# Scaled fp16 projections in a two-layer diffusion backbone: values, queries and keys, and two loads moved

## The chip, the cores and the metric

The kernel runs as one program on 1 core of one Trainium2 chip. The metric is the time of one execution on the device, in microseconds (us). TensorE (PE) multiplies matrices into PSUM; VectorE (DVE) and ScalarE (ACT) do the elementwise work and move results out of PSUM; GpSimd (POOL), SyncE (SP) and ACT issue DMA transfers. Each engine works through its own list of instructions in the order in which the program holds them.

## The reference: what is computed

Two layers over 1024 latent tokens and 256 context tokens of width 1024, in float32. Layer 0 mixes tokens with Fourier groups and a Hyena convolution, layer 1 with neighbourhood attention of 16 heads; both end in a SwiGLU of width 2816. The lines that bear on this change:

```python
def swiglu(u, w_gate, w_up, w_down):
    return (jax.nn.silu(u @ w_gate) * (u @ w_up)) @ w_down

def mixer_na(u_lat, u_ctx, w_qkv, w_out, rpb, with_ctx_out):
    heads = lambda t: t.reshape(t.shape[0], t.shape[1], NA_HEADS, NA_HEAD_DIM)
    q, k, v = (heads(t) for t in jnp.split(u_lat @ w_qkv, 3, axis=-1))
    kc, vc = (heads(t) for t in jnp.split(u_ctx @ w_qkv[:, D_MODEL:], 2, axis=-1))
    y_lat = neighbourhood_attention(q, k, v, kc, vc, rpb).reshape(B_, L, D_MODEL) @ w_out
```

In layer 1, `u_lat` and `u_ctx` are the normalised and modulated streams, `rms_norm(h) * (1 + scale) + shift`. Its context output isn't needed, so context tokens have keys and values there, and no queries.

## The kernel before, in words

**Two parts for each operand.** A matrix product is made of three: an operand is split into a high part, rounded to a shorter format, and a low part, the rest; high by high, high by low and low by high are added up in PSUM. In most of the kernel both parts are `float32r` (`split`, L352 on ACT and L354 on DVE). The feed-forward products use fp16 parts instead (`split_scaled`, L1885 and L1886): weights and activations are first multiplied by factors that keep them in fp16's range, found from the largest absolute values (`scan` and `bound` sum absolute values on ACT, `scale_x`, `scale_w` and a reduction over partitions on POOL make the factor), and the results are multiplied by the inverse.

**Stages in order of time.** (1) Layer 0's mixer and its output projection. (2) Layer 0's feed-forward: context's gate and up products, then the latent ones by a Winograd-like scheme of 7 products for 2 by 2 blocks (`wino_steps`, matmuls on L2032), in 11 groups `i`, each with one gate and one up matrix pair. (3) `down` for layer 0: seven passes `p` over 11 operand pairs (matmuls on L2279), then context's own down product, 22 steps `kb` of 24 matmuls (L2401). (4) `values`: V for 10 blocks of tokens, 4 weight tiles `kp` for each of four accumulation groups. (5) `attention`: 64 items (a head, half the rows, two column chunks) in three stages each (scores, transposes of the probabilities, the product with V), with `attn_prep` of the next pair of heads woven between them: K for latent and context tokens and Q, 24 matmuls for each of 5 pieces. All of their matmuls go through the helper at L348. (6) The output projection, layer 1's feed-forward and `down`.

**What sets the order.** A tile framework records the program and a list scheduler orders each engine's instructions; buffers come from pools (21 tiles of 4 KB a partition in `p4`, 35 of 2 KB in `p2`, 4 of tag `ws` for staged weights, two each of tags `wh` and `wl` for split ones, the last also used as four `hl` tiles, each holding both fp16 parts). `follow(x)` tells the scheduler to place what comes next after instruction `x`; `next(g)` in the loops takes the next piece of a side job `g`.

**Around the change.** In the feed-forward's group `i`, `sums` (L2085) loads four tiles of the down weights and makes from them the four sums that Winograd needs, writes them to DRAM (L2093 to L2096) and bounds them (L1965, ACT). `ahead` is a `scan` over layer 1's gate and up weights (L1854 on ACT, loads on ACT's queue, L336), four pieces to a group. In `down`, `operands` (L2257) loads two tiles, 256 KB each, and splits them (L2269 ACT, L2270 DVE); `mark` (L2342) remembers the last load and split of pass 5, and context's down weights (512 KB each, L2394) are placed behind `mark`. Plain loads are issued by SP (L333), spills by POOL (L339).

## Time and profile before

| what | value |
|---|---|
| time, median of 3 runs | 2844.2 us (2842.24 to 2845.08) |
| profiled execution, its own time | 2844.23 us |
| its span in the trace | 2842.5 us |
| mean granted TensorE clock | 0.982 |
| busy: PE, PE weight loads, DVE, ACT, POOL | 2722.5, 1839.6, 2128.6, 1594.8, 508.4 us |
| feed-forward of layer 0, latent part | 913 to 1318 us |
| `down` of layer 0, seven passes / context's part | 1318 to 1538 / 1538 to 1598 us |
| `values` | 1598 to 1708 us |
| attention with its projections | 1708 to about 2180 us |
| feed-forward of layer 1 and `down` | 2234 to 2842 us |

A row of a matmul in the trace lasts from its start to its modelled end, so rows overlap: what a stream of matmuls costs is the distance from start to start. Weight loads (PEld) run beside matmuls. Some matmul records are missing from a trace, above all for fp16, where weight loads are instructions of their own and are counted in full. "landed" is when a DMA's data had arrived. "`<-`" behind idle time names what ended it.

### The profile page before, as it was taken

What the parts mean: (1) busy time and instruction counts of PE and PEld (TensorE: products, weight loads), DVE (VectorE), ACT (ScalarE), POOL (GpSimd) and SP (SyncE); (2) the same over time, 40 slices, a digit from 0 to 9 for tenths busy, and PEclk for the clock granted to TensorE, in tenths of its full rate; (3) what the DMA queues carried; (4) which work ended last, traced back from release to release, by engine and by line L of the source; (5) the groups of instructions that cost most, each with busy time, mean ns of one, the idle gap of its engine ahead of it and who ended that gap; (6) DMA issues with size and microseconds to landing.
All of it is one profiled execution on the core that took longest, in us unless ns stands there. A gap on an engine that the chain in (4) does not pass through costs nothing. (4 is left out here: it accounts for less than half of the span.)

```text
span 2842.5 us, 44453 instructions
## 1 busy us (share of the span) xinstructions
PE 2722.5 (96%) x15570; PEld 1839.6 (65%) x15570; DVE 2128.6 (75%) x3849; ACT 1594.8 (56%) x2957; POOL 508.4 (18%) x817
## 2 busy tenths in 40 slices
PE   6999889999999999999999999999999999999998
PEld 3877677888898444444445888888887544444444
DVE  5678788868877898886897736777787876776774
ACT  3533334543488665666656526778775555565653
POOL 2110223351100011112021002323222012221000
PEclk9999899999999999999999999999999999999999
DMA  7344726766645677787997436878775245655872
GB/s 264 99 159 144 220 93 196 230 200 221 227 165 181 236 270 255 255 320 265 372 318 241 134 115 162 191 187 199 188 261 171 101 142 202 219 207 178 291 231 97
DMA packets 308862, 583.34 MB, mean 205 GB/s; under 512 B 82968, under 2 KB 129754, under 8 KB 308638
## 3 DMA queue, kind: packets, MB, share of 16 engines
q1 hardware_dynamic: 241374, 378.61, 42.1%
q0 software_dynamic: 53760, 158.38, 16.0%
q10 hardware_dynamic: 13504, 43.52, 4.4%
q8 instruction: 122, 2.00, 0.3%
q14 instruction: 102, 0.84, 0.1%
HBM read 433.05 MB, written 119.80 MB: 194 GB/s over the span
## 5 line engine op out<-in xcount | busy, mean ns | idle before, releaser
L2032 PE MATMUL ps<-s,s 128*128 128x512 f16 x2280 | 512.5, 379 | 11.3 <-ACT g L2037 3.3
L2032 PEld LDWEIGHTS <-s 128*128 128x128 f16 x2640 | 257.9, 98 | 327.2 <-issue 16.4
L348 PE MATMUL ps<-s,wh 128*128 128x256 f32 (+1 forms) x1784 | 408.8, 332 | 8.7 <-ACT wh L352 6.0
L348 PEld LDWEIGHTS ps<-s,wh 128*128 128x128 f32 x1784 | 298.5, 191 | 44.3 <-ACT wh L352 8.7
L2279 PE MATMUL ps<-s 128*128 128x512 f16 (+2 forms) x1404 | 321.4, 380 | 5.9 <-ACT s L2269 5.9
L2279 PEld LDWEIGHTS <-s 128*128 128x128 f16 x1716 | 167.1, 98 | 205.5 <-issue 12.4
L348 PE MATMUL ps<-s,wl 128*128 128x256 f32 (+1 forms) x892 | 271.3, 330 | 3.9 <-DVE wl L354 3.9
L2269 ACT ACTIVATE s<-s,c 128x512 f16<-128x512 f32 (+1 forms) x300 | 199.9, 715 | 115.4 <-DMA s<-d 67.8
L348 PE MATMUL pq<-s,wh 128*128 128x512 f32 (+1 forms) x840 | 256.6, 385 | 0.4 <-ACT wh L352 0.4
L348 PE MATMUL ps<-s,s 128*128 128x65 f16 (+4 forms) x2748 | 230.9, 235 | 15.3 <-DMA s<-tk 7.6
L2270 DVE SCALAR_TENSOR_TENSOR s<-s,c,s 128x512 f16<-128x512 f32 (+1 forms) x300 | 210.3, 749 | 45.2 <-ACT s L2269 44.6
L339 POOL DMA_DIRECT2D d<-s x245 | 133.1, 544 | 521.3 <-DVE s L1744 86.1
L2032 PE MATMUL ps<-s,hl 128*128 128x512 f16 x924 | 214.6, 379 | 1.3 <-ACT hl L1885 1.3
L2032 PEld LDWEIGHTS <-hl 128*128 128x128 f16 x1056 | 103.2, 98 | 126.0 <-ACT hl L1885 1.5
L348 PEld LDWEIGHTS ps<-s,wl 128*128 128x128 f32 x892 | 166.7, 190 | 22.6 <-DVE wl L354 5.7
L354 DVE TENSOR_TENSOR wl<-ws,wh 128x1024 fp32r<-128x1024 f32 (+1 forms) x84 | 99.5, 1187 | 89.0 <-ACT wh L352 84.7
L348 PEld LDWEIGHTS pq<-s,wh 128*128 128x128 f32 x840 | 150.5, 190 | 22.8 <-ACT wh L352 1.0
L348 PE MATMUL pq<-s,wl 128*128 128x512 f32 (+1 forms) x420 | 159.3, 380 | 0.0
L352 ACT CAST wh<-ws 128x1024 fp32r<-128x1024 f32 (+1 forms) x84 | 84.5, 1010 | 132.9 <-PE ps L348 82.8
L348 PEld LDWEIGHTS ps<-s,s 128*128 128x128 f32 (+1 forms) x828 | 130.3, 193 | 25.0 <-issue 3.4
L1886 DVE SCALAR_TENSOR_TENSOR s<-t,c,s 128x512 f16<-128x512 f32 x176 | 128.1, 746 | 10.1 <-ACT s L1885 10.1
L1885 ACT ACTIVATE s<-t,c 128x512 f16<-128x512 f32 x176 | 118.6, 713 | 6.0 <-DVE t L2011 4.5
(534 smaller groups left out, 5239.3 us busy)
## 6 DMA issues: line engine op xcount, KB each, us to landing
s<-d SPq DMA_DIRECT2D x326, 256.0 KB, 4.9
d<-s POOLq DMA_DIRECT2D x229, 256.0 KB, 3.5
s<-in_down SPq DMA_DIRECT2D x150, 256.0 KB, 5.6
ws<-in_gate SPq DMA_DIRECT2D x42, 512.0 KB, 4.1
ws<-in_up SPq DMA_DIRECT2D x42, 512.0 KB, 4.8
s<-in_ada_w POOLq DMA_DIRECT2D x34, 512.0 KB, 7.0
d<-s SPq DMA_DIRECT2D x60, 256.0 KB, 2.3
s<-in_ada_w ACTq DMA_DIRECT2D x30, 512.0 KB, 7.7
```

Of the source, the lines that this page charges most:

```text
L339: self.last_ldr = self.nc.gpsimd.dma_start(out, in_).ins
L348: self.last_mm = self.nc.tensor.matmul(o, l, r, start=st, stop=sp).ins
L352: self.last_hi = nc.scalar.copy(hi, src).ins
L354: self.last_lo = eng.tensor_tensor(lo, src, hi.bitcast(F32), SUB).ins
L1885: self.last_hi = self.nc.scalar.activation(hi, src, AF.Copy, scale=s).ins
L1886: self.last_lo = self.nc.vector.scalar_tensor_tensor(lo, src, s, hi, op0=MUL, op1=SUB).ins
L2032: nc.tensor.matmul(ps, x[:, sl], y, start=first and j == 0 and x is wh and y is xh, stop=j == 3 and x is wl, skip_group_check=True)
L2269: self.last_hi = nc.scalar.activation(x, f[:, c:c + 512], AF.Copy, scale=s).ins
L2270: self.last_lo = nc.vector.scalar_tensor_tensor(y, f[:, c:c + 512], s, self.raw_part(x), op0=MUL, op1=SUB).ins
L2279: m = nc.tensor.matmul(acc[j][:, c0:c1], x[:, sl], y[:, xs], start=first and k == 0, stop=last and k == 2, skip_group_check=True)
```

## The change

Three things are done.

1. **V, K and Q are projected from fp16 parts.** The normalised stream of layer 1 (`u1`) is held in fp16 (`new_act16`) and scaled by a factor for the latent and one for the context stream (`scale_u`, made at the end of layer 0's feed-forward from the modulation's rows). The weights `wv`, `wk` and `wq` are split by `weights16` into fp16 parts with a factor each (`scale_p`). For those factors the absolute values of the weights are summed: `wv`'s 8 tiles behind the 44 of `ahead` in layer 0's feed-forward (five pieces to a group instead of four; `up.to(3)` is split off from `up.to(5)` for the fifth), `wk`'s and `wq`'s 16 tiles in `values`, two pieces to each weight tile. The copies out of PSUM multiply by the inverse factors.
2. **Loads for the sums of down's weights** are recorded between the first and second half of the gate's steps, and their arithmetic stays at the group's end, in both layers.
3. **`mark` is taken in pass 6** instead of pass 5: context's down weights are placed behind the last operands of the whole of `down`.

```diff
+    def new_act16(self, pc, b):
+        act = Act()
+        w = WID[pc]
+        t = self.S4(F16, 2048) if pc < 2 else self.S2(F16, 1024)
+        for k in range(4):
+            act.put(k % 2, b + k // 2, pc, t[:, k * w:k * w + w])
+        return act
...
-    def scan(self, key, tiles):
+    def scan(self, tiles, mark):
...
-            with self.follow(self.last_ev):
+            with self.follow(mark()):
                 if k > 1:
-                    nc.scalar.activation(t, t, AF.Abs, accum_out=sums[:, k - 2:k - 1])
+                    nc.scalar.activation(t, t, AF.Abs, accum_out=tiles[k - 2][1])
                 if k < n:
-                    self.lda(t, tiles[k])
+                    self.lda(t, tiles[k][0])
...
+    def scale_u_begin(self):
+        nc = self.nc
+        t = self.cw[:, 20:28]
+        for c in (0, 1):
+            for j in (0, 1):
+                nc.vector.tensor_reduce(t[:, 2 * j + c:2 * j + c + 1], self.ada[(1, c)][:, j * 8:j * 8 + 8], axis=AX, op=MAX,
+                                        apply_absolute_value=True)
+        nc.gpsimd.partition_all_reduce(t[:, 4:8], t[:, 0:4], channels=P, reduce_op=bass.bass_isa.ReduceOp.max)
+        return t
...
+    def scale_p(self, sums, maxes, names, c0):
+        nc = self.nc
+        nc.gpsimd.partition_all_reduce(maxes, sums, channels=P, reduce_op=bass.bass_isa.ReduceOp.max)
...
+    def weights16(self, src, s):
+        st = self.W("ws", "ws")
+        self.ld(st, src)
+        return self.split_scaled(st, self.hl(), s)
...
-        def sums(i):
+        def sums_load(i):
...
+            return t
+
+        def sums(i, t):
+
+            a21, a22, a11, a12 = t
...
-            ahead = self.scan("next", [a[x][1, fb] for x in ("gate", "up") for fb in range(NFB)])
+            sums2 = self.wsc["next"] = self.C(4 * NFB)
+            src = [a[x][1, fb] for x in ("gate", "up") for fb in range(NFB)]
+            ahead = [(x, sums2[:, k:k + 1]) for k, x in enumerate(src)]
+            ahead += [(a["wv"][k // 4, k % 4], self.cws[:, k:k + 1]) for k in range(8)]
+            ahead = self.scan(ahead, lambda: self.last_ev)
...
             g.to(5)
             up.to(1)
+            ks = (2 * i - 6, 2 * i - 5) if l == 1 else (9, 10) if i == 9 else (i,) if i < 9 else ()
+            ks = [(k, sums_load(k)) for k in ks if 0 <= k < n2]
             next(ahead, None)
             g.to(7)
...
+            up.to(3)
+            next(ahead, None)
             up.to(5)
             next(ahead, None)
...
-                if p == 5 and i == n2 - 1:
+                if l == 0 and p == 1 and i == 9:
+                    with self.follow(self.last_lo):
+                        self.scale_p(self.cws[:, 0:8], self.cws[:, 8:16], (("v", 1.0),), 32)
+                if p == 6 and i == n2 - 1:
                     mark = self.last_ld, self.last_hi, self.last_lo
...
-                    wh, wl = self.weights(a["wv"][ch, kp])
+                    wh, wl = self.weights16(a["wv"][ch, kp], self.wsc["v"][0])
...
-            self.aw = self.weights(a["wk"][0])
+            self.aw = self.weights16(a["wk"][0], self.wsc["k"][0])
...
-                    wq = self.weights(a["wq"][pr])
+                    wq = self.weights16(a["wq"][pr], self.wsc["q"][0])
...
-                nc.scalar.copy(dst[own], acc[pc][own, :w])
-                nc.vector.tensor_tensor(dst[other], acc[pc][own, :w], dst[own].bitcast(F32), SUB)
+                s = self.wsc["k"][2 if pc == 2 else 1][own]
+                nc.scalar.activation(dst[own], acc[pc][own, :w], AF.Copy, scale=s)
+                nc.vector.scalar_tensor_tensor(dst[other], acc[pc][own, :w], s, dst[own].bitcast(F32), op0=MUL, op1=SUB)
...
+        qk = self.scan([(a[x][k], self.cws[:, c + k:c + k + 1]) for x, c in (("wk", 16), ("wq", 24)) for k in range(8)],
+                       lambda: self.last_hi)
         for i, _ in enumerate(self.values(u1)):
...
+            for _ in range(2 if i < 9 else 0):
+                next(qk)
```

How the order of instructions moves, at three places. The first is SP's queue at the turn from pass 5 to pass 6 of `down` in layer 0. `s<-in_down` and `s<-d` are the two halves of an operand pair, `ws<-in_down 128x2x512` is one step's weights for context. Before:

```order
L333 DMA s_3128_14292<-d_7511 128x512
L333 DMA s_3128_14292<-d_7466 128x512
L333 DMA ws_14600<-in_down 128x2x512
L333 DMA ws_14643<-in_down 128x2x512
L333 DMA ws_14676<-in_down 128x2x512
L333 DMA ws_14719<-in_down 128x2x512
L333 DMA s_3130_14312<-in_down 128x512
L333 DMA s_3130_14312<-d_7397 128x512
L333 DMA ws_14798<-in_down 128x2x512
L333 DMA ws_14831<-in_down 128x2x512
L333 DMA s_3132_14320<-in_down 128x512
L333 DMA s_3132_14320<-d_7404 128x512
```

After the change the 11 operand pairs of pass 6 follow pass 5's last one directly, and then the context weights; of the pairs the first two and the last two are shown:

```order
L333 DMA s_3128_14323<-d_7511 128x512
L333 DMA s_3128_14323<-d_7466 128x512
L333 DMA s_3130_14343<-in_down 128x512
L333 DMA s_3130_14343<-d_7397 128x512
L333 DMA s_3132_14351<-in_down 128x512
L333 DMA s_3132_14351<-d_7404 128x512
...
L333 DMA s_3157_14551<-in_down 128x512
L333 DMA s_3157_14551<-d_7460 128x512
L333 DMA s_3160_14560<-in_down 128x512
L333 DMA s_3160_14560<-d_7467 128x512
L333 DMA ws_14631<-in_down 128x2x512
L333 DMA ws_14673<-in_down 128x2x512
```

Eight context loads, four of them ahead of pass 6's first operand, have moved behind its last.

The second is SP's queue in one group of layer 0's feed-forward, before:

```order
L333 DMA ws_10210<-in_up 128x1024
L333 DMA ws_10212<-in_up 128x1024
L333 DMA ws_10459<-in_gate 128x1024
L333 DMA s_2515_10079<-in_down 128x512
L333 DMA s_2516_10080<-in_down 128x512
L333 DMA s_2517_10081<-in_down 128x512
L333 DMA s_2518_10082<-in_down 128x512
L333 DMA s_2519_10099<-d_7514 128x512
L333 DMA ws_10461<-in_gate 128x1024
```

and after:

```order
L333 DMA ws_10216<-in_up 128x1024
L333 DMA ws_10218<-in_up 128x1024
L333 DMA s_2510_9991<-in_down 128x512
L333 DMA s_2511_9992<-in_down 128x512
L333 DMA s_2512_9993<-in_down 128x512
L333 DMA s_2513_9994<-in_down 128x512
L333 DMA ws_10467<-in_gate 128x1024
L333 DMA s_2519_10105<-d_7514 128x512
L333 DMA ws_10469<-in_gate 128x1024
```

The four loads for the sums stand ahead of the next group's first gate load, where they stood behind it.

The third is ACT's list at the start of `values` after the change: `hl<-ws` (here L1933) is the high part of a `wv` tile, `s<-in_wk` a load for the sums over `wk`, and L1862 such a sum.

```order
L336 DMA s_3279_15501<-in_wk 128x1024
L336 DMA s_3280_15502<-in_wk 128x1024
L1933 ACTIVATE hl_15507<-ws_15505,c_317 128x1024
L1862 ACTIVATE s_3279_15501,c_319<-s_3279_15501 128x1024
L1862 ACTIVATE s_3280_15502,c_319<-s_3280_15502 128x1024
L336 DMA s_3279_15501<-in_wk 128x1024
L1933 ACTIVATE hl_15558<-ws_15556,c_317 128x1024
L336 DMA s_3280_15502<-in_wk 128x1024
L1862 ACTIVATE s_3279_15501,c_319<-s_3279_15501 128x1024
```

Before the change nothing but splits of weights, copies and the norm's work stood there.

More of the change, by code (lines that the diff above doesn't have):

```diff
@@ L684, in norm_block @@
         nc.scalar.activation(hi, t[:, :w], AF.Identity, bias=sh)
[L685 removed]
+        nc.vector.scalar_tensor_tensor(lo, t[:, :w], sh, self.raw_part(hi), op0=ADD, op1=SUB)
     def norm(self, h, pcs, l, m, act):
@@ L1842, in scale_x @@
         self.xinv = t[:, 0:1]
-    def scan(self, key, tiles):
+    def scan(self, tiles, mark):
         nc = self.nc
         n = len(tiles)
-        sums = self.C(2 * n)
         st = [self.S4() for _ in range(2)]
@@ L1851, in scan, with scale_u @@
             t = st[k % 2]
-            with self.follow(self.last_ev):
+            with self.follow(mark()):
                 if k > 1:
-                    nc.scalar.activation(t, t, AF.Abs, accum_out=sums[:, k - 2:k - 1])
+                    nc.scalar.activation(t, t, AF.Abs, accum_out=tiles[k - 2][1])
                 if k < n:
-                    self.lda(t, tiles[k])
+                    self.lda(t, tiles[k][0])
             yield
-        self.wsc[key] = sums
+    def scale_u_begin(self):
[7 more added lines that the diff above has]
+        return t
+    def scale_u(self, t):
+        nc = self.nc
+        self.uinv = self.cw[:, 28:30]
+        s = self.cw[:, 30:32]
+        nc.vector.scalar_tensor_tensor(self.uinv, t[:, 6:8], 32.0, t[:, 4:6], op0=MUL, op1=ADD)
+        nc.vector.tensor_scalar(self.uinv, self.uinv, 1e-30, 1.0 / 8192.0, op0=MAX, op1=MUL)
+        nc.vector.reciprocal(s, self.uinv)
+        for c in (0, 1):
+            ad = self.ada[(1, c)][:, :16]
+            nc.vector.tensor_scalar(ad, ad, s[:, c:c + 1], None, op0=MUL)
+    def scale_p(self, sums, maxes, names, c0):
+        nc = self.nc
+        nc.gpsimd.partition_all_reduce(maxes, sums, channels=P, reduce_op=bass.bass_isa.ReduceOp.max)
+        for j, (k, f) in enumerate(names):
+            t = self.cw[:, c0 + 4 * j:c0 + 4 * j + 4]
+            nc.vector.tensor_reduce(t[:, 0:1], maxes[:, 8 * j:8 * j + 8], axis=AX, op=MAX)
+            nc.vector.tensor_scalar(t[:, 0:1], t[:, 0:1], 1e-30, 1.0 / 8192.0, op0=MAX, op1=MUL)
+            nc.vector.reciprocal(t[:, 1:2], t[:, 0:1])
+            nc.vector.tensor_scalar(t[:, 2:4], self.uinv, t[:, 0:1], f, op0=MUL, op1=MUL)
+            self.wsc[k] = t[:, 1:2], t[:, 2:3], t[:, 3:4]
+    def weights16(self, src, s):
+        st = self.W("ws", "ws")
+        self.ld(st, src)
+        return self.split_scaled(st, self.hl(), s)
     def either(self, x):
@@ L2152, in bounds @@
         def bounds(i, ts):
+            nonlocal us
             for j, t in enumerate(ts):
@@ L2159, in bounds @@
             hidden.clear()
+            if i == n2 - 2 and l == 0:
+                us = self.scale_u_begin()
             if i == n2 - 2:
@@ L2165, in ffn @@
         self.junk = self.S2(mybir.dt.bfloat16)
-        hidden = []
+        hidden, us = [], None
         prev = None
@@ L2219, in ffn @@
                 nc.vector.reciprocal(dsc, inv)
+                if l == 0:
+                    with self.follow(add):
+                        self.scale_u(us)
             prev = (up, gate)
-            for k in (2 * i - 6, 2 * i - 5) if l == 1 else (9, 10) if i == 9 else (i,) if i < 9 else ():
-                if 0 <= k < n2:
-                    sums(k)
+            for k, t in ks:
+                sums(k, t)
                 if l == 0:
@@ L2435, in values @@
                     t = self.T()
-                    nc.scalar.copy(t, acc[tb])
+                    nc.scalar.activation(t, acc[tb], AF.Copy, scale=self.wsc["v"][2 if tb >= 8 else 1])
                     nc.vector.tensor_reduce(mx[:, ch * 10 + tb:ch * 10 + tb + 1], t, axis=AX, op=MAX,
@@ L2524, in attn_prep @@
                 if pc == 1 and i == 3 and pr < 7:
-                    nxt = self.weights(a["wk"][pr + 1])
+                    nxt = self.weights16(a["wk"][pr + 1], self.wsc["k"][0])
                 yield s
@@ L2529, in attn_prep @@
                 qh, ql = self.S2(F32R), self.S2(F32R)
-                nc.scalar.mul(qh[own], acc[pc][own], 0.125)
-                nc.vector.scalar_tensor_tensor(ql[own], acc[pc][own], 0.125, qh[own].bitcast(F32), op0=MUL, op1=SUB)
+                s = self.wsc["q"][1][own]
+                nc.scalar.activation(qh[own], acc[pc][own], AF.Copy, scale=s)
+                nc.vector.scalar_tensor_tensor(ql[own], acc[pc][own], s, qh[own].bitcast(F32), op0=MUL, op1=SUB)
                 for t in (qh, ql):
@@ L2860, in after2 @@
                 if b % 2 == 0:
-                    u1.t.update(self.new_act(pcs=(pc,), blocks=(b, b + 1)).t)
+                    u1.t.update(self.new_act16(pc, b).t)
                 self.norm_block({b: h3.ap(0, b, pc)}, b, pc, 1, 0, u1, r)
@@ L2872, in run @@
                 next(self.last, None)
-            if i in (8, 10):
+            for _ in range(2 if i < 9 else 0):
+                next(qk)
+            if i in (8, 10, 12):
                 with self.follow(self.last_lo):
@@ L2876, in run @@
                         self.scale_x(1, 3)
+                    elif i == 10:
+                        self.scale_p(self.cws[:, 16:32], self.cws[:, 32:48], (("k", 1.0), ("q", 0.125)), 36)
                     else:
```

2 lines of the change are left out of this document (removed).

## The prediction

> **What bounds the kernel now.** I read the windows by stage first, then for each stage what ended TensorE's idle time, then the timeline for the distance from matmul to matmul.
>
> ```profile
> PE 2722.5 (96%) x15570; PEld 1839.6 (65%) x15570; DVE 2128.6 (75%) x3849; ACT 1594.8 (56%) x2957; POOL 508.4 (18%) x817
> 913.00:1318.00 405.00, 393.90 (x1812) 176.93 (x1813) 342.53 (x633) 260.10 (x518) 62.48 (x116) 1.00 0.74 263
> 1318.00:1538.00 220.00, 214.09 (x969) 102.36 (x967) 179.87 (x322) 125.58 (x195) 32.44 (x61) 0.98 0.89 317
> 1598.00:1708.00 110.00, 110.00 (x491) 91.11 (x489) 48.41 (x86) 36.84 (x57) 0.37 (x1) 1.00 0.38 123
> 1734.00:2140.00 406.00, 391.97 (x3758) 350.11 (x3756) 318.58 (x701) 310.16 (x708) 114.52 (x188) 1.00 0.78 197
> ```
>
> The columns after the stretch and its length are PE, PEld, DVE, ACT and POOL busy, the granted clock, the DMA share and GB/s. In `values` (1598 to 1708) PE is never idle and everything else is lightly used; in attention PE is idle for 14 of 406 us. So a matmul that is shortened there shortens the path, as long as the other engines keep up: DVE and ACT are at 78% and 76% in attention. The feed-forward is PE's too, with 11 us of idle time.
>
> **Context's down weights.** The one large hole in PE's work in this half of the kernel lies at the start of pass 6:
>
> ```profile
> 1499.68 1.24 PE L2279 MATMUL ps<-s 128*128 128x512 f16 x5
> 1504.64 5.28 PE L2279 MATMUL ps<-s 128*128 128x512 f16 x12 [3.72 <-ACT s L2269]
> 1511.93 1.02 PE L2279 MATMUL ps<-s 128*128 128x512 f16 x4 [2.01 <-ACT s L2269]
> 1512.79 0.98 PE L348 MATMUL pq<-c,tk 128*128 128x1 f32 x8
> ACT s L2269 <- DMA s<-in_down: 5.8, 2, 5.1
> 1477.89 2.12 SPq L333 DMA_DIRECT2D ws<-in_down  x4
> 1480.10 0.65 SPq L333 DMA_DIRECT2D s<-in_down  x1
> 1488.64 3.26 SPq L333 DMA_DIRECT2D ws<-in_down  x2
> 1497.49 0.42 SPq L333 DMA_DIRECT2D s<-in_down  x1
> ws<-in_down SPq DMA_DIRECT2D x8, 512.0 KB, 11.1
> 2597.69 2.75 PE L2032 MATMUL ps<-s,s 128*128 128x512 f16 x12
> 2600.28 4.91 PE L2032 MATMUL ps<-s,hl 128*128 128x512 f16 x22
> ```
>
> PE waits for ACT's split, which waits for the operand's load, which SP issued behind context loads of 512 KB; those took 11.1 us to land, and SP could issue the third pair only at 1497.49. An fp16 matmul of 512 columns costs 0.216 us: 12 between 2597.69 and 2600.28. The last of the five at 1499.68 is done by about 1500.8; until 1512.79 there are 16 matmuls, 3.5 us of work. The hole is 12.0 - 3.5 = **8.5 us**. With the context loads behind pass 6's last operand its cause is gone. What is late next would be context's first weights. Pass 5's last operand was issued ahead of 1477.89, 23 us before the pass ended at 1500.8. Pass 6 takes 132 x 0.216 = 28.5 us from there, to 1529; at the same lead its last pair is issued about 1506, and the context loads follow, some 20 us ahead of context's first matmul. I take the full 8.5 us; the low end is 4, should half of the wait return at 1530.
>
> **V, K and Q.** The cost now, from the first matmul of a stretch to that of the next:
>
> ```profile
> 1653.37 0.61 PE L348 MATMUL ps<-wh,s 128*128 128x512 f32 x2
> 1656.77 0.61 PE L348 MATMUL ps<-wh,s 128*128 128x512 f32 x2
> 1707.99 0.62 PE L348 MATMUL pq<-s,wh 128*128 128x512 f32 x2
> 1718.65 0.39 PE L348 MATMUL pq<-s,wl 128*128 128x512 f32 x1
> 1718.88 0.40 PE L348 MATMUL pq<-s,wh 128*128 128x256 f32 x2
> 1721.63 0.28 PE L348 MATMUL pq<-s,wl 128*128 128x256 f32 x1
> 1721.86 0.71 PE L348 MATMUL pq<-s,wh 128*128 128x512 f32 x2
> 1733.42 0.63 PE L348 MATMUL pq<-s,wh 128*128 128x512 f32 x2
> 1563.28 21.12 PE L2401 MATMUL ps<-s,hl 128*128 128x256 f16 x192
> ```
>
> V: 15 matmuls in 3.40 us, 0.2267 each. K: 47 steps in 10.66 us, 0.2268. K of context: 23 steps of 256 columns in 2.75 us, 0.1196. Q, whose moving operand is read in pieces of 16 columns: 48 in 11.56 us, 0.2408. In fp16 the first two should cost 0.216, the third 0.110 (192 in 21.1 us). The trace has no fp16 stream read in pieces of 16; Q can gain nothing (0.2408 again) or all (0.216), and I take K's gain of 11 ns, since the pieces should cost fp16 what they cost now.
> V: 480 x 10.8 ns = 5.2 us. K: 8 x 48 x 11 ns = 4.2. Context's K: 8 x 24 x 9.6 ns = 1.8. Q: 384 x 11 ns = 4.2 (0 to 9.5). Together **15.4 us** (11.2 to 20.7).
>
> [...]
>
> The weight loads that become instructions of their own, 1440, run beside the matmuls:
>
> ```profile
> L348 PEld LDWEIGHTS ps<-wh,s x224: 187/188/192, 1598.1 to 1707.5; 128*128 128x128 f32 x112
> L2401 PEld LDWEIGHTS <-hl x528: 95/98/181, 1538.9 to 1598.0; 128*128 128x128 f16 x176
> PE ps L348 <- DMA s<-tk: 7.6, 9, 1.6
> ```
>
> At 98 ns (188 now) they are hidden even behind context's 0.110 us steps. Where attention goes from short matmuls to a projection, a load of 188 ns shows partly; 56 times 90 ns less bounds that gain at 5 us, and I take 2. Against it stands the wait of PE for the transposed probabilities (7.6 us in attention): their DMA takes as long as before, and each item gets 15.4 - 5.2 = 10 us / 64 = 0.16 us shorter, so the 9 waits grow by 1.5 us. These two leave 0.5 us. Splits and copies become instructions of about the same length, and hide as they do now.
>
> **The sums over the weights.**
>
> ```profile
> L1854 ACT ACTIVATE s<-s x44: 1043/1056/1067, 941.4 to 1331.9; 128x1024 f32<-128x1024 f32 x44
> s<-in_gate ACTq DMA_DIRECT2D x22, 512.0 KB, 7.4
> ws<-in_wv SPq DMA_DIRECT2D x11, 512.0 KB, 3.6
> ```
>
> 24 more at 1.06 us on ACT, each behind a load. In `values` 16 of them make 17 us on an ACT that is busy for 37 of 110, so the work fits; the order is the risk. Two stand between one `wv` split and the next, and block ACT until their loads land, 3.6 us on quiet queues and 7.4 beside the feed-forward. PE needs a weight tile each 24 x 0.216 = 5.2 us in the first two groups. Splits are up to three tiles ahead, 15 us. At 3.6 us plus two sums, 5.7 a tile, ACT falls behind by 0.5 us a tile, which the lead covers; at 7.4, 9.5 a tile, it loses 4.3 x 8 = 34 us in 8 tiles, less the lead 19. I take 1 us between 0 and 19, nearer to the quiet end, since DMA is at 0.38 there.
> By the Trainium skill, "DMA: Bandwidth & Descriptors", Issuing engines are not separate DMA queues, ACT's loads share the 16 DMA engines with SP's, so another queue buys no room. The longer landings beside the feed-forward agree.
>
> **The feed-forward of layer 0.** PE's waits there are small and many:
>
> ```profile
> PE ps L2032 <- ACT g L2037: 3.3, 3, 1.5
> PE ps L2032 <- ACT s L2037: 3.0, 6, 0.8
> PE ps L2032 <- DVE s L2056: 2.7, 4, 0.9
> DVE s L2093 <- DMA s<-in_down: 9.3, 6, 3.9
> 1089.79 0.33 SPq L333 DMA_DIRECT2D ws<-in_gate  x1
> 1090.22 3.47 SPq L333 DMA_DIRECT2D s<-in_down  x4
> 1105.58 5.44 SPq L333 DMA_DIRECT2D ws<-in_up  x2
> ```
>
> PE waits for copies out of PSUM that stand behind other work on ACT and DVE. SP sits on the gate load until a `ws` buffer is free (1089.79) with the sums' four loads behind it; ahead of it they are issued some 20 us earlier, DVE's 9.3 us of waiting for them goes, and less collides with the gate and up loads. ACT gets 8 more sums and a fifth step a group, 8.5 us on 260 of 405. A gain can be at most the 9 us of these waits, a loss at most those 8.5 us in full; I take a gain of 1. Layer 1's group has hardly a wait to remove: 0. The factors (a few small DVE operations, three reductions on POOL) lie beside splits that run 20 us ahead: 0.
>
> **Sum**, against the profiled execution's 2844.2 us (span 2842.5), which is the median of the runs: 8.5 + 15.4 + 0.5 - 1 + 1 = 24.4, so **2820 us**.
>
> **Rivals.** (a) *Attention isn't paced by PE.* DVE and ACT, at three quarters, and the DMA of the transposes set its pace, and the projections' 10 us there turn into waits. What remains is 8.5 + 5.2 = 13.7: 2830. For it: the 78%; against: 14 us of idle PE in 406. (b) *Values starve* behind the sums, 8 us of the 19: 2828. (c) *More than the rows promise*: Q gains all of 9.5, the feed-forward loses 5 us of its waits: 2844.2 - 24.4 - 5.3 - 4 = 2810. (d) *Slower*: SP's queue in the feed-forward. If the sums' four tiles get no `p2` buffer until the last group's sums are spilled, SP waits on them and the gate load behind comes late in each of 10 groups. From 2.5 us of late weights a group the gain is eaten; at 4 us the kernel takes 2820 + 40 = 2860. Against it: in the row at 1090.22 the four were issued without a wait as soon as SP reached them. (e) *The projections keep their steps*, since float32r streams a column as fast as fp16: 2844.2 - 8.5 - 0.5 = 2835; the V rows, 10.8 ns above fp16's, speak against it. [...]
>
> **Chances.** Forecast 0.52, (a) 0.18, (b) 0.10, (c) 0.12, (d) 0.04, (e) 0.04. The range 2808 to 2833 takes in (a), (b) and (c) with their costs and leaves out (d) and (e). Within 0.2% (5.7 us), about what a measurement of this kernel can tell from no change, end only mixtures of (d): faster 0.93, same 0.03, slower 0.04.
>
> **What would show it.** Right: no idle PE ahead of pass 6; V at 0.216 from matmul to matmul, K too, and Q at 0.22 to 0.24; `values` in some 105 us and attention's stretch some 10 shorter. Wrong: PE waiting for `hl` in `values` with ACT behind a sum's load (b); PE's idle time in attention up by as much as the projections fell (a); gate weights late in the feed-forward (d); a wait at context's first matmul. The total is wrong if either the 8.5 us hole reopens elsewhere or fp16 steps don't reach 0.216.

## The result and the profile after

The changed kernel takes **2814.1 us** (median of 4 runs, 2812.7 to 2817.0) against 2844.6 for the kernel before on the same chip (4 runs, 2842.2 to 2850.9): a ratio of **0.9891, 95% interval 0.9872 to 0.9909**. The forecast was 2820 in a range of 2808 to 2833. The profiled execution's span fell by 31.6 us, from 2842.5 to 2810.8. Two executions of the kernel before, of 5318 and 9471 us on the chip of the first four experiments, are left out of every figure here.

Lines have moved: the feed-forward's matmuls stand on L2080 now (L2032 before), those of `down` on L2344 (L2279), its operands' splits on L2334 (L2269), attention's transposes on L2703 (L2633), their high and low parts on L2706 and L2707 (L2636, L2637). In an experiment's kernel a line can stand one or two off these.

The table cuts the span into stages, each from the start of its first row to the start of the next stage's, read from the two traces:

| stage | before | after | change | forecast |
|---|---|---|---|---|
| up to the feed-forward's first latent matmul | 913.9 | 912.3 | -1.6 | 0 |
| feed-forward of layer 0 | 403.9 | 397.4 | -6.5 | -1 |
| `down` of layer 0, seven passes | 221.1 | 210.3 | -10.7 | -8.5 |
| context's part of `down` | 59.1 | 59.1 | 0 | 0 |
| V, and the preparation of pair 0, to the first transpose | 149.5 | 144.1 | -5.4 | -5.5 |
| attention, first to last transpose | 405.4 | 397.1 | -8.3 | -9.4 |
| to the feed-forward of layer 1 | 70.9 | 71.5 | +0.6 | 0 |
| feed-forward and `down` of layer 1 | 618.7 | 618.9 | +0.2 | 0 |

(V's forecast is 5.2 + an eighth of the 10.2 us for K and Q, less 1 for the sums; attention's is seven eighths of those 10.2 and the 0.5 for weight loads and waits. In the kernel before, layer 1's feed-forward begins at 2223.8 us, not at the 2234 of the stage table ahead of the change; no term of the forecast hangs on it.)

The page's line of busy time and the windows by stage, with the columns as before:

```profile
PE 2695.3 (96%) x15570; PEld 1717.7 (61%) x15570; DVE 2129.7 (76%) x3870; ACT 1631.0 (58%) x3005; POOL 514.1 (18%) x820
```

```profile
912.00:1310.00 398.00, 392.58 (x1813) 177.18 (x1814) 344.25 (x643) 272.27 (x543) 67.63 (x119) 1.00 0.78 280
1310.00:1520.00 210.00, 210.00 (x971) 101.88 (x969) 178.49 (x324) 121.57 (x186) 32.48 (x60) 1.00 0.93 328
1580.00:1685.00 105.00, 103.28 (x481) 47.12 (x480) 51.16 (x94) 54.05 (x87) 0.95 (x2) 1.00 0.61 200
1709.00:2110.00 401.00, 382.13 (x3768) 283.61 (x3765) 317.17 (x702) 319.00 (x711) 115.83 (x191) 1.00 0.80 198
```

PE is without a gap in `down` (210.00 of 210.00; 214.09 of 220 before). In `values` it waits for 1.7 us, where it waited for nothing. In attention it is idle for 19 us of 401, where it was for 14 of 406: PE's work fell by more than the stretch did.

**The hole ahead of pass 6 is gone.** The timeline of PE there, and of SP's queue, in the changed kernel:

```profile
1489.64 11.40 PE L2344 MATMUL ps<-s 128*128 128x512 f16 x52
1500.88 0.95 PE L348 MATMUL pq<-c,tk 128*128 128x1 f32 x8
1501.68 9.66 PE L2344 MATMUL ps<-s 128*128 128x512 f16 x44
1496.07 0.38 SPq L333 DMA_DIRECT2D s<-in_down  x1
1497.50 14.57 SPq L333 DMA_DIRECT2D ws<-in_down  x7
1520.05 5.20 PE L2469 MATMUL ps<-s,hl 128*128 128x256 f16 x46
```

The first half of the last operand pair is issued at 1496.07 and context's weights from 1497.50 on, 22 us ahead of context's first matmul at 1520.05, which doesn't wait. The gain is larger than the 8.5 us of the hole, though. The kernel before shows why: first its timeline in the rest of pass 6, then two windows ahead of it and in it, where the granted clock is the number behind the five engines:

```profile
1513.63 16.52 PE L2279 MATMUL ps<-s 128*128 128x512 f16 x68
1529.99 1.02 PE L348 MATMUL pq<-t,c 128*128 128x512 f32 x2
```

```profile
1504.60:1509.30 4.70, 4.66 (x12) 1.57 (x11) 4.70 (x10) 1.26 (x2) 0.00 (x0) 0.50 0.75 238
1513.00:1517.00 4.00, 4.00 (x16) 1.89 (x17) 3.28 (x6) 3.98 (x7) 0.00 (x0) 0.62 0.92 294
```

After the wait of 3.72 us the granted clock was 0.50, and 12 matmuls took 5.28 us. After the second wait it was 0.62 once more, beyond the point at which the forecast's sum ended: the 68 matmuls behind it took 16.36 us from 1513.63 to 1529.99, against 68 x 0.216 = 14.7. That is 1.7 us more, 10.2 with the 8.5. By the Trainium skill, "TensorE: Matmul & The Clock Gate", What's actually happening, the array falls to half its clock after an idle window of about 3.4 us; here it fell after waits of 3.72 and of 2.01 us, so a shorter wait can be enough.

**The fp16 steps.** PE's timeline in V, in K with context's K, and in Q of pair 0:

```profile
1631.36 1.46 PE L348 MATMUL pq<-hl,s 128*128 128x512 f16 x6
1632.65 6.64 PE L348 MATMUL ps<-hl,s 128*128 128x512 f16 x30
1639.13 1.46 PE L348 MATMUL pq<-hl,s 128*128 128x512 f16 x6
1685.75 13.14 PE L348 MATMUL pq<-s,hl 128*128 128x512 f16 x72
1699.33 10.53 PE L348 MATMUL pq<-s,hl 128*128 128x512 f16 x48 [0.44 <-DVE s L2587]
```

V: 36 matmuls in 7.77 us, 0.2158 each. K: 48 matmuls of 512 columns and 24 of 256 in 13.1 us with the last one's end, where 48 x 0.216 + 24 x 0.110 make 13.0. Q: 48 in 10.53 us, of which the last one's modelled end is 0.38: 47 steps in 10.15, **0.216**. So Q's reading in pieces of 16 columns costs fp16 nothing; float32r had paid some 12 ns a step for it, as an experiment below shows. Q gained all of the 9.5 us that were the upper bound, not 4.2.

**Attention, cut in three.** The first 48 items use the transposing DMA, the next 8 don't and still have projections beside them, the last 8 have the output projection. Windows of the kernel before, cut at the last transposes of the 48th and of the 56th item:

```profile
1747.00:2044.00 297.00, 289.37 (x2801) 259.39 (x2800) 232.00 (x515) 232.69 (x536) 95.06 (x148) 1.00 0.82 191
2044.00:2093.00 49.00, 46.79 (x485) 41.78 (x484) 38.53 (x92) 35.95 (x88) 10.54 (x21) 1.00 0.88 272
2093.00:2153.00 60.00, 55.08 (x527) 47.74 (x525) 47.87 (x101) 40.30 (x91) 9.79 (x18) 0.97 0.55 180
```

and of the changed one:

```profile
1723.00:2009.00 286.00, 278.76 (x2799) 201.38 (x2798) 228.80 (x511) 238.82 (x535) 94.07 (x148) 1.00 0.85 198
2009.00:2061.00 52.00, 45.44 (x484) 36.08 (x483) 39.16 (x92) 37.10 (x88) 11.24 (x22) 1.00 0.87 250
2061.00:2120.00 59.00, 53.94 (x519) 46.76 (x518) 47.45 (x100) 40.18 (x89) 9.78 (x18) 0.97 0.56 183
```

In the first stretch PE's work fell by 10.6 us and the stretch by 11: everything came through. In the second, PE's work fell by 1.4 us and the stretch *grew* by 3. What PE waited for longest there in the changed kernel (line waited for, us in total, times, longest), and then its timeline: four of the waits, and the one instruction of ACT behind the longest:

```profile
PE ps L348 <- DVE st L2686: 2.4, 1, 2.4
```

```profile
2017.46 0.81 PE L348 MATMUL ps<-s,s 128*128 128x65 f16 x21 [1.85 <-DMA s<-tk]
2038.61 1.07 PE L348 MATMUL ps<-s,s 128*128 128x65 f16 x30 [2.44 <-DVE st L2686]
2047.63 0.59 PE L348 MATMUL ps<-s,s 128*128 128x384 f32 x2 [0.82 <-DVE s L2707]
2053.98 0.59 PE L348 MATMUL ps<-s,s 128*128 128x384 f32 x2 [0.57 <-DVE s L2744]
2036.99 0.51 ACT L2565 ACTIVATE s<-t,c 128x256 f16<-128x256 f32 x1 [4.38 <-DMA t<-d]
```

ACT stands for 4.38 us before a block of values whose load has not landed (`value`, L2565); DVE's low part of it waits for ACT, the item's maxima (L2686) stand behind that on DVE, and PE ends up waiting 2.44 us. The wait of 1.85 us is for the transposing DMA of an item ahead of this stretch. The two waits of score matmuls (384 columns) for DVE's L2707 and L2744 can be read as waits for a PSUM tile that DVE is still reading, since these matmuls read nothing that DVE writes there. That the stretch grew isn't chance: from the 48th to the 56th item's last transpose the six traces with all fp16 products in this order and 48 items on the transposing DMA took 51.7 to 54.9 us, and the three with float32r in the same order 48.9 to 51.3.

### The profile page after: what moved, and what is told of

The parts are those of the page before. It is cut to its first block, busy times and chain, and to the rows that moved or that the text cites. A ratio compares the mean times of both kernels' runs of the same rounds, so it can differ in the third digit from the quotient of the medians.

```text
span 2810.8 us, 44489 instructions
## 1 busy us (share of the span) xinstructions
PE 2695.3 (96%) x15570; PEld 1717.7 (61%) x15570; DVE 2129.7 (76%) x3870; ACT 1631.0 (58%) x3005; POOL 514.1 (18%) x820
## 5 line engine op out<-in xcount | busy, mean ns | idle before, releaser
L2080 PE MATMUL ps<-s,s 128*128 128x512 f16 x2280 | 508.9, 379 | 5.6 <-DVE s L2104 3.1
L2080 PEld LDWEIGHTS <-s 128*128 128x128 f16 x2640 | 258.0, 98 | 320.5 <-issue 10.1
L2344 PE MATMUL ps<-s 128*128 128x512 f16 (+2 forms) x1404 | 316.1, 376 | 0.2 <-ACT s L2334 0.2
L2344 PEld LDWEIGHTS <-s 128*128 128x128 f16 x1716 | 166.1, 98 | 196.1 <-issue 5.3
L2334 ACT ACTIVATE s<-s,c 128x512 f16<-128x512 f32 (+1 forms) x300 | 199.9, 714 | 118.7 <-DMA s<-d 63.0
L348 PE MATMUL ps<-s,s 128*128 128x65 f16 (+4 forms) x2748 | 242.4, 238 | 19.3 <-DMA s<-tk 5.0
L2080 PE MATMUL ps<-s,hl 128*128 128x512 f16 x924 | 212.2, 379 | 1.2 <-ACT hl L1933 1.2
L348 PE MATMUL pq<-s,hl 128*128 128x512 f16 (+1 forms) x960 | 206.9, 358 | 0.4 <-DVE s L2587 0.4
L2080 PEld LDWEIGHTS <-hl 128*128 128x128 f16 x1056 | 103.2, 98 | 125.9 <-ACT hl L1933 1.4
L1933 ACT ACTIVATE hl<-ws,c 128x1024 f16<-128x1024 f32 x89 | 101.8, 1144 | 107.8 <-DMA ws<-in_up 37.7
L1934 DVE SCALAR_TENSOR_TENSOR hl<-ws,c,hl 128x1024 f16<-128x1024 f32 x89 | 114.0, 1283 | 62.6 <-ACT hl L1933 62.3
L348 PEld LDWEIGHTS <-s 128*128 128x128 f16 x2400 | 115.2, 98 | 66.8 <-DMA s<-tk 5.7
L348 PEld LDWEIGHTS <-hl 128*128 128x128 f16 x960 | 86.8, 98 | 80.3 <-issue 8.8
L1933 ACT ACTIVATE s<-t,c 128x512 f16<-128x512 f32 x176 | 118.1, 714 | 9.2 <-DVE t L2059 5.6
```

The source lines that it names most:

```text
L348: self.last_mm = self.nc.tensor.matmul(o, l, r, start=st, stop=sp).ins
L1933: self.last_hi = self.nc.scalar.activation(hi, src, AF.Copy, scale=s).ins
L1934: self.last_lo = self.nc.vector.scalar_tensor_tensor(lo, src, s, hi, op0=MUL, op1=SUB).ins
L2080: nc.tensor.matmul(ps, x[:, sl], y, start=first and j == 0 and x is wh and y is xh, stop=j == 3 and x is wl, skip_group_check=True)
L2334: self.last_hi = nc.scalar.activation(x, f[:, c:c + 512], AF.Copy, scale=s).ins
L2344: m = nc.tensor.matmul(acc[j][:, c0:c1], x[:, sl], y[:, xs], start=first and k == 0, stop=last and k == 2, skip_group_check=True)
```

## The experiments

They ran on several chips, each beside runs of the kernel before on its own chip, to which its ratio is taken; those runs scatter more here than in the first comparison (2836 to 2856, medians 2844.5 to 2848.3). The stages are read from each kernel's trace as in the table above:

| kernel | feed-forward 0 | `down` 0 | V, pair 0 | attention | first 48 items | to layer 1's feed-forward |
|---|---|---|---|---|---|---|
| before | 403.9 | 221.1 | 149.5 | 405.4 | 296.6 | 70.9 |
| after | 397.4 | 210.3 | 144.1 | 397.1 | 285.7 | 71.5 |
| mark in pass 5 | 398.5 | 220.5 | 146.7 | 401.0 | 288.8 | 71.2 |
| sums' loads late | 398.0 | 210.7 | 144.8 | 400.2 | 285.5 | 71.3 |
| four pieces a group | 401.1 | 219.4 | 143.8 | 395.0 | 282.9 | 73.8 |
| projections only | 398.3 | 220.8 | 144.4 | 396.6 | 283.7 | 70.3 |
| before, Q read flat | 399.6 | 224.2 | 148.9 | 408.5 | 299.4 | 71.6 |
| no low part of wq | 398.7 | 210.4 | 145.5 | 412.1 | 299.8 | 74.1 |
| no sums over wk, wq | 399.0 | 210.4 | 142.5 | 395.2 | 284.0 | 73.8 |
| before, five pieces | 399.3 | 222.5 | 149.5 | 406.7 | 295.5 | 70.7 |
| values' products later | 399.2 | 210.3 | 144.2 | 411.0 | 288.3 | 71.7 |
| no low part, and later | 402.3 | 210.4 | 140.2 | 401.6 | 276.1 | 72.0 |
| before, later | 399.6 | 222.9 | 149.5 | 413.9 | 292.7 | 72.4 |
| DMA transposes for 56 | 399.5 | 210.3 | 143.9 | 403.1 | 286.8 | 70.7 |

### The mark alone

```diff
-                if p == 6 and i == n2 - 1:
+                if p == 5 and i == n2 - 1:
```

> The changed kernel with context's down weights put back behind pass 5's last operand. Theory: these loads alone made the hole ahead of pass 6, so TensorE waits there for 8 to 9 us again and the kernel takes 2814 + 8.5 = 2822 to 2825 us, with the stretch from pass 1 to pass 7 about 10.7 us longer than in the changed kernel. Rival: the hole was closed by the smaller fp16 tiles of the normalised stream, which leave more buffers for pass 6's operands; then the stretch stays at about 210 us and the kernel within 2 us of 2814.

Measured: 2823.4 us (2820.7 to 2831.6), ratio 0.9907 (0.9876 to 0.9938). `down` is back at 220.5, and PE's waits in it are back:

```profile
PE ps L2344 <- ACT s L2334: 7.0, 3, 3.9
```

The mark is worth 10.2 us in `down`; the ratios of the whole, 0.9907 and 0.9891, have intervals that overlap and don't show it by themselves. In the six traces with the mark in pass 5 `down` takes 220.5 to 224.2; with the mark in pass 6 and five pieces a group it takes 210.3 to 210.7.

### The sums' loads

```diff
-            ks = [(k, sums_load(k)) for k in ks if 0 <= k < n2]
...
-            for k, t in ks:
-                sums(k, t)
+            for k in [k for k in ks if 0 <= k < n2]:
+                sums(k, sums_load(k))
```

> The changed kernel with the loads for the sums of down's weights back at the group's end. Theory: the feed-forward of layer 0 became 6.5 us shorter because these loads moved, so 5 to 6.5 us come back there: 2819 to 2821 us. Rival: the gain came from the fifth step a group (the up product's steps split in two), and this kernel stays within 1.5 us of 2814.

Measured: 2816.1 us (2814.5 to 2817.7), ratio 0.9884 (0.9849 to 0.9919). The feed-forward takes 398.0 with the loads late and 397.4 with the loads early. That the 6.5 us come from these loads falls: they bring nothing that can be measured.

### Four pieces a group, and both load moves undone

```diff
-            up.to(3)
-            next(ahead, None)
             up.to(5)
```

> The changed kernel with the up product's steps not split and the sums over the next weights at four pieces a group, the last ones after the groups. Theory (the loads made the feed-forward's gain): within 2 us of 2814, or a few us slower where the 10 left-over sums, at 1.25 us, delay the first splits of the down product. Rival (the split made it): 5 us slower in the groups' stretch, 2819 us.

Measured: 2826.4 us (2824.6 to 2836.4), ratio 0.9938 (0.9908 to 0.9969). The feed-forward takes 401.1, 3.7 us more, and `down` 9 more, by one wait in its second pass:

```profile
PE ps L2342 <- ACT s L2332: 6.8, 1, 6.8
```

Without the fifth piece ten sums are left over when the groups end; their loads and sums stand on ACT ahead of the splits of `down`'s operands, and ACT waits up to 3.8 us for one of these loads.

> The changed kernel with both moves of loads undone, so that only the fp16 projections with their sums over the weights are left. Theory: the three parts add up. Of the 31.6 us the feed-forward's 6.5 and down's 10.7 come back: 2814 + 17 = 2831 us, with values and attention as short as in the changed kernel (13.7 us less than before). Rival: the parts lean on each other, and the sum differs from the single ones by more than 3 us.

This is the changed kernel with both edits above (mark in pass 5, sums' loads at the group's end). Measured: 2827.5 us (2820.6 to 2836.6), ratio 0.9928 (0.9905 to 0.9952). `down` is at 220.8, V and attention keep their gain, and the feed-forward stays at 398.3. So the parts add up by stage, and what shortened the feed-forward is in neither load move.

### Is it the fifth piece?

```diff
             next(ahead, None)
+            up.to(3)
+            next(ahead, None)
             up.to(5)
```

in the kernel before, with nothing else of the change:

> The kernel before, with five pieces of the scan over layer 1's weights in each group of layer 0's feed-forward instead of four (the up step is split in two, and the scan of 20 tiles is done two groups earlier); no other part of the change. If the fifth piece and the order that the scheduler makes of it are what shortened the feed-forward in the changed kernel, its stretch falls from 403.9 to some 398 to 400 us and the whole by 4 to 6 us, ratio about 0.998. If the gain belongs to the parts of the change that stay undone here (which would be the sums over wv or the scale of layer 1's input), the stretch stays at 403 to 404.

Measured: 2839.9 us (2833.0 to 2850.1), ratio 0.9982 (0.9965 to 0.9999), and a feed-forward of 399.3: just what the theory said. Yet it isn't shown. The next experiment below leaves each engine's order of instructions as in the kernel before, in the feed-forward and everywhere, and its feed-forward took 399.6. PE's longest waits there, in the profile of the kernel before and in the one with Q read flat:

```profile
PE ps L2032 <- ACT g L2037: 3.3, 3, 1.5
PE ps L2032 <- ACT s L2037: 3.0, 6, 0.8
PE ps L2032 <- DVE s L2056: 2.7, 4, 0.9
```

```profile
PE ps L2032 <- DVE s L2056: 2.6, 3, 1.7
PE ps L2032 <- ACT g L2037: 1.5, 2, 0.9
PE ps L2032 <- ACT s L2037: 1.3, 2, 0.9
```

The same list of instructions waits for 11.7 us in one execution and 7.6 in the other. The kernel before with the values' products later, which differs only in attention, had 399.6 too. So some 4.3 of the 6.5 us belong to that one execution (or its chip), and the change's own part is 0 to 2 us, which these traces can't tell from none: 399.6 against 397.4 to 399.5 in the traces with its groups (402.3 once). Where the ratio of 0.9982 comes from isn't settled; the kernel's stages are shorter by 0.3 in the feed-forward and by 1.7 in `down` than those of the kernel with Q read flat, and its attention is longer by 1.3 than the kernel before's, which nothing in the edit explains and which are the size of the scatter.

### Q's pieces of 16 columns

```diff
-            for i, s in enumerate(lin(*wq, pc, acc, by_chunk)):
+            for i, s in enumerate(lin(*wq, pc, acc)):
```

> The kernel before, with Q's moving operand read in its stored order instead of in pieces of 16 columns (so the columns of q come out in another order, and the output differs). If the pieces are what made a float32r step of Q cost 0.2408 us, Q's 48 steps now take 0.2267 each, like V and K: 10.9 us a pair instead of 11.6, and attention's stretch is up to 384 x 14 ns = 5.4 us shorter. If Q's step is long for another reason, it stays at 0.2408 and attention stays as it was (405 us).

Measured, in one run: 2843.4 us. Q's matmuls:

```profile
1717.81 0.70 PE L348 MATMUL pq<-s,wh 128*128 128x512 f32 x2
1728.81 0.62 PE L348 MATMUL pq<-s,wh 128*128 128x512 f32 x2
```

From Q's first to the next pair's first there are 48 steps in 11.00 us, 0.2292 each, where the pieces took 0.2408, counted alike. So the pieces were the cause of some 12 of the 14 ns; the rest lies in the first steps of Q's stretch, which are longer with and without pieces, and from the fourth on the step is 0.2272, close to the 0.2267 of V and K. By the Trainium skill, "Advanced Engine Details and Errata", SBUF Cachelines, what a stride costs depends on the type; here it costs float32r 12 ns in 229 and fp16 nothing. Attention's stretch didn't follow: it took 408.5, and PE's waits for the transposing DMA went from 7.6 to 10.7 us. What PE saves here goes in part into that wait.

### How much of PE's saving comes through?

```diff
-                for w, part in ((wh, 0), (wh, 1), (wl, 0)):
+                todo = ((wh, 0), (wh, 1), (wl, 0)) if low else ((wh, 0), (wh, 1))
+                for n, (w, part) in enumerate(todo):
...
-            for i, s in enumerate(lin(*wq, pc, acc, by_chunk)):
+            for i, s in enumerate(lin(*wq, pc, acc, by_chunk, False)):
```

> The changed kernel without Q's products with the low part of wq (128 of 384 matmuls left out, so q is less exact): 128 x 0.216 = 27.6 us of TensorE's work go, 7/8 of it, 24.2 us, within attention's stretch. If attention is TensorE's, the stretch falls from 397 to about 373 us; if DVE, ACT or the DMA of the transposed probabilities set its pace (rival a), it falls by 5 us or less and TensorE's idle time grows by the rest. The share that comes through here is a measure of the share of the fp16 steps' saving that can come through.

Measured, in one run: 2831.8 us, *slower* than the changed kernel with 27.6 us less of work for PE; attention took 412. One run can't show the whole to be slower (runs of one kernel lie up to 20 us apart on one chip here), but 412 is 9 us above the longest that this stretch took in any trace with all fp16 products in the same order. The windows from first to last transpose, of the changed kernel first, then of this one, with its longest wait, and a short window behind one of these waits:

```profile
1723.00:2120.00 397.00, 378.13 (x3798) 284.22 (x3797) 315.42 (x701) 316.09 (x710) 115.09 (x187) 1.00 0.81 203
```

```profile
1724.00:2137.00 413.00, 368.46 (x3694) 283.44 (x3693) 320.84 (x702) 316.43 (x712) 115.68 (x187) 0.96 0.79 195
```

```profile
PE ps L348 <- DMA s<-tk: 22.9, 15, 2.8
```

```profile
1766.00:1770.00 4.00, 4.00 (x33) 3.14 (x34) 2.22 (x5) 1.67 (x4) 1.15 (x1) 0.60 0.95 269
```

PE is idle for 44.5 us instead of 18.9, 25.7 more: the whole saving of 24.2 turned into waits. And the work that is left takes 368.5 us, where 378.1 - 24.2 = 353.9 were to be expected: 14.6 us more, with the granted clock at 0.96 over the stretch and at 0.60 in the 4 us behind a wait of 2.77. So idle time costs twice: -24.2 + 25.7 + 14.6 = +16, and that is what the stretch grew by. The granted clock accounts for the 14.6: in this stretch the trace has nine spans at half clock, 34.1 us in all, against one of 3.4 in the changed kernel, and half of the difference is 15.4 us (an estimate, since part of it fell into waits). The transposing DMA itself was slower too: its median from issue to landing was 3.9 us in the kernel before, 4.7 in the changed one and 5.3 here. It looks as if attention had no slack left with fp16 projections: the chain of one item (scores, exponentials, transposing DMA, products with the values) takes as long as the work that is put beside it. The next two kernels test this.

### The products with the values an item later

```diff
-                i = k - ahead - stage
+                i = k - ahead - (0, 1, 3)[stage]
...
-        for it in items[-2:]:
+        for it in items[-3:]:
```

> The changed kernel with an item's products with the values issued one item later, so that the transposed probabilities have some 6 us more to arrive before TensorE's queue reaches them; nothing is left out. Theory: attention is paced in part by the chain of one item (scores, exponentials, transposes, the transposing DMA), which is late at the end: TensorE's waits for the DMA into s (5.0 us) and for DVE's low parts of transposed probabilities (4.0) go, and attention's stretch falls from 397 to some 388 to 393 us; the whole to 2805 to 2811. Rival: the waits come from tiles that are held, and holding them an item longer moves the waits to the scores: attention stays at 395 to 401 or grows.

Measured: 2833.4 us (2831.0 to 2840.0), ratio 0.9964 (0.9952 to 0.9976), so 0.7% slower than the changed kernel's ratio. Waits, and two rows of PE's timeline:

```profile
PE ps L2703 <- ACT t L2688: 13.0, 2, 11.1
PE ps L348 <- DVE s L2744: 11.1, 11, 2.3
```

```profile
2103.41 0.69 PE L2703 MATMUL ps<-c,t 128*128 128x128 f32 x2 [11.05 <-ACT t L2688]
1943.00 0.70 PE L348 MATMUL ps<-s,s 128*128 128x384 f32 x2 [2.31 <-DVE s L2744]
```

The waits for the transposing DMA are gone, all 5.0 us. In their place scores wait 11.1 us for PSUM tiles that DVE's L2744 reads (1.4 in the changed kernel): the waits moved to the scores, as the rival had it, though which tiles are short isn't shown. And the last items, with no work beside them, leave PE idle for 11 us at a stretch; from the 56th item's last transpose on, 10 of the 14 us are lost. The first 48 items took 288.3, against 285.7: nothing gained even there.

> Both: without Q's products with the low part of wq (27.6 us of TensorE's work less) and the products with the values one item later. Without the second, the stretch took 412 us with TensorE waiting 22.9 us for the transposing DMA. If the chain of one item is what stopped it, the stretch is now TensorE's again: 397 - 24 = 373, up to 380 with the rest of the waits. If ACT or DVE (at 80% of the time in the changed kernel) or the DMA engines set the pace by their throughput, it stays above 390.

Measured, in one run: 2823.2 us, attention 401.6, the first 48 items 276.1, which is 12.2 less than with the low part (288.3). Over the whole stretch 9.4 of the 24.2 us come through now, where nothing did. So the item's chain was a stop, and behind it stands the next one: scores that wait for DVE's reads of PSUM.

```profile
PE ps L348 <- DVE s L2745: 12.0, 12, 1.4
```

By the number, 401.6, the rival holds (above 390), and the theory's 373 to 380 falls. But throughput is not shown to be the reason: DVE and ACT were busy for 229 and 239 of the first 276 us, and the last items take 10 us longer here, too, than in the changed kernel.

> The kernel before with the products with the values one item later; nothing is left out. Theory: its 7.6 us of waits for the transposing DMA go, attention falls from 405 to some 396 to 399, ratio about 0.997; then the fp16 steps would bring some 12 to 14 us between this kernel and e9, against 8.3 between the two as they were. Rival (held tiles): no gain, 405 or more.

Measured: 2853.1 us (2842.7 to 2860.1), ratio 1.0023 (1.0004 to 1.0041). Here, too, the waits for the DMA go, the first 48 items gain 4 us, and the last sixteen lose 12, most of it in one wait of 10.9 us at the end. The theory falls for the whole stretch: in this form the order in time of the kernel before is the better one.

### The sums over wk and wq

```diff
-        qk = self.scan([(a[x][k], self.cws[:, c + k:c + k + 1]) for x, c in (("wk", 16), ("wq", 24)) for k in range(8)],
-                       lambda: self.last_hi)
+        nc.vector.memset(self.cws[:, 16:32], 32.0)
+        qk = iter(())
...
-                next(qk)
+                next(qk, None)
```

> The changed kernel without the 16 sums over wk and wq during values (a constant 32 stands where their results were, so the scale of k and q's weights is fixed and not taken from the data). My theory: they cost 0 to 2 us (the 1.7 us wait of TensorE on ACT in values goes), V and its preparation in 142 to 144 us instead of 144.1, and the whole within 0.1% of the changed kernel. Rival (b): 8 us or more faster.

Measured: 2814.4 us (2813.0 to 2818.1), ratio 0.9889 (0.9864 to 0.9914). V and pair 0's preparation take 142.5, 1.6 us less, and the whole is where the changed kernel is. With the sums and all products this stretch took 143.8 to 146.7 over the traces, so the sums cost about what the forecast took for them, give or take 2 us; values don't starve.

### Eight more items on the transposing DMA

```diff
-                                         osb, pr if hd == 1 and c0 == 2 else None, 8 * pr + 4 * hf + 2 * hd + c0 // 2 < 48)
+                                         osb, pr if hd == 1 and c0 == 2 else None, 8 * pr + 4 * hf + 2 * hd + c0 // 2 < 56)
```

> The changed kernel with the transposing DMA for 56 of the 64 items instead of 48 (items 48 to 55 lose 4 of their 10 TensorE transposes, a copy out of PSUM on ACT and a subtraction on DVE, and gain a copy on ACT, a subtraction on POOL and a DMA); nothing is left out. Items 48 to 55 took 49 us in the kernel before and take 52 in the changed one, with 6.6 us of idle TensorE. Theory: these items are paced by ACT and DVE, on which the fp16 steps save nothing; with less work there they take 46 to 49 us, attention's stretch 391 to 395, the whole 2808 to 2812. Rival: in that stretch the DMA engines are at 0.87 and 250 GB/s with the output projection's weights on SP's queue, and the transposing DMAs come late: 52 us or more, and the whole no faster or slower.

Measured: 2823.2 us (2813.2 to 2834.0), ratio 0.9906 (0.9882 to 0.9930). The rival holds: items 48 to 55 take 57 us. Window of their first 52 us, the wait, and its longest piece:

```profile
2014.00:2066.00 52.00, 42.29 (x420) 32.97 (x418) 31.85 (x76) 34.15 (x79) 16.26 (x25) 0.90 1.00 245
```

```profile
PE ps L348 <- DMA s<-tk: 11.4, 4, 5.5
```

```profile
2043.18 1.33 PE L348 MATMUL ps<-s,s 128*128 128x65 f16 x21 [5.49 <-DMA s<-tk]
```

The DMA engines are at 1.00 there, and PE waits 11.4 us. DVE and ACT have less to do, and it doesn't help; whether they alone would have set the pace at 52 us isn't told by this. No version here is measurably faster than the changed kernel.

## Why the prediction was right, and where its terms were off

The total, the sign and the main places were right; the forecast was 6 us too high. By its own steps:

- **The hole, 8.5 us: right in its cause, mis-sized.** It measured 10.7 between the two profiles and 10.2 in the kernel with only the mark put back. The sum ended at 1512.79 and took the 68 matmuls behind the second wait at 0.216; they ran at 0.2406, since the clock was at 0.62 after that wait. That is the missing 1.7. Half of the wait did not return at 1530, for the reason that the forecast gave: the last pair was issued 24 us ahead of context's first matmul, where the same lead as before, 23 us, was expected (the clock times differ by the 8 us that the stages ahead had saved).
- **V 5.2, K 4.2, context's K 1.8: right.** 0.2158 a step, and K's 72 matmuls in 13.1 us. Of the rival in which float32r streams as fast as fp16 nothing is left.
- **Q 4.2: mis-sized.** The step was "the pieces should cost fp16 what they cost now". They cost it nothing, and Q gained 9.5. With the pieces taken away in float32r the step was 0.2292 instead of 0.2408, which names them as the cause.
- **Attention's 9.4 us: nearly right, by two errors that cancel.** With Q's 9.5, seven eighths of 15.5 = 13.6 us of PE's work went (13.1 by the busy time in the windows); 8.3 us came through, a figure good to some 3 us, since over the six traces with these projections in this order and 48 items on the transposing DMA the stretch took 395.0 to 401.0. In the first 48 items all of it did (11 us); in the next 8 the stretch grew by 3, where ACT stood before a late block of values, and products waited for the transposing DMA and scores for PSUM tiles. So rival (a), PE doesn't pace attention, is true of items 48 to 55, and for the rest, in this order, it becomes true just below the changed kernel's length: a further 24.2 us less of work made the stretch 15 us longer. The argument against it, 14 us of idle PE in 406, measured how much PE was used, not how much slack the item's chain had.
- **The 0.5 us for weight loads and waits** can't be told apart. Their step "their DMA takes as long as before" failed (4.7 us to landing in the median, 3.9 before), and yet the wait for it fell from 7.6 to 5.0 where 9.1 was expected; new waits for PSUM tiles and values took its place.
- **The sums in `values`, 1 us: right as far as can be told.** The stretch was 1.6 shorter without them, which is about its scatter, and the whole no different.
- **The feed-forward, 1 us: as far as can be told, right.** The 6.5 us of the two profiles looked like the rival "more than the rows promise"; but the same instructions took 403.9 in one execution and 399.6 in another. The loads that were moved ahead have no part in it. The 1.6 us ahead of the feed-forward are scatter too: this stretch took 910 to 920 us over all the traces.

Between the two profiles 31.6 us went, 7.2 more than forecast: 5.5 of these in the feed-forward and 1.6 ahead of it (mostly scatter), 2.2 in `down`; attention, the stretch behind it and the rest took 2 back.

## What to carry to other kernels

A wait of 2 to 4 us can cost more than its length, since the matmuls behind it can run at half the clock for 3.4 us or a multiple of that: count the distance from start to start until the step is back at its full rate. A busy PE at 96% doesn't tell how much of a saving on it will come through; take a larger piece of its work away and see, for here the first 13.6 us brought 8.3 and the next 24 brought a loss. And before a stage's change is put down to an edit, look for two executions of one order of instructions in that stage: here they differed by 4.3 us in 404, and an expectation that came true to the number was no proof.

## What was not expected of the hardware

Float32r pays 12 ns in 229 for a moving operand read in pieces of 16 columns, and fp16 pays nothing. The clock's fall after a wait isn't a matter of the wait's length alone: without the low part of wq, it was at 0.60 behind a wait of 2.77 us, and in the changed kernel at 1.00 behind one of 2.44, while in the kernel before it fell behind one of 2.01. The traces' records of the clock show why. In each trace every change of it falls on a grid of 3.41 us, and a span at half clock lasts one or more steps of that grid. Three steps in a row of the kernel before, the first of them double:

```profile
1503.71:1510.54 6.83, 5.28 (x12) 1.68 (x12) 6.54 (x12) 3.32 (x6) 0.00 (x0) 0.50 0.82 272
1510.54:1513.95 3.41, 2.02 (x14) 1.49 (x15) 3.31 (x6) 3.34 (x6) 0.00 (x0) 1.00 1.05 398
1513.95:1517.36 3.41, 3.41 (x10) 1.22 (x8) 2.69 (x5) 3.41 (x7) 0.00 (x0) 0.50 0.89 270
```

The wait of 2.77 us lay almost whole in one step, 1763.39 to 1766.80, in which PE was busy for 0.80 us; the wait of 2.44 us lay half in each of two steps of the changed kernel:

```profile
2034.03:2037.44 3.41, 2.14 (x15) 1.51 (x14) 0.00 (x0) 0.45 (x1) 0.00 (x0) 1.00 1.07 295
2037.44:2040.86 3.42, 2.25 (x37) 1.63 (x37) 2.95 (x8) 2.95 (x8) 0.94 (x2) 1.00 0.61 151
```

From 1200 to 2600 us of the 14 traces, of the steps at full clock in which PE was busy for less than 45%, all 48 were followed by one at half clock; between 45 and 65% it was 10 of 81, and above 65% none of 5521 (from 100 to 2790 us, 21 of 10,351). So a step need not be idle throughout for the clock to fall. A window of activity that runs on its own, as the Trainium skill has it ("TensorE: Matmul & The Clock Gate", What's actually happening), fits this grid.
